# Three feed-forward stages of a hybrid trunk in two phases: first projection by seven block products, second summed in eight banks

## The chip, the cores and the metric

The kernel runs on one core of one Trainium2 chip. The metric is the time of one execution on the device, in microseconds (us). Engines: TensorE (PE, matmuls; PEld its weight loads), VectorE (DVE), ScalarE (ACT), GpSimd (POOL), and SyncE (SP), which here only issues DMAs.

## The reference

Two layers of a trunk over 512 latent tokens and 256 context tokens with width 1024; every layer has a half-step feed-forward network (FFN), a merge of a Fourier and a state-space (S5) branch, and a second half-step FFN. Layer 1 drops the context after its merge, so its last FFN has 512 tokens. Three FFNs have all 768.

```
def swiglu(h, w13, w2):
    a, b = jnp.split(h @ w13, 2, axis=-1)
    return (jax.nn.silu(a) * b) @ w2

def half_ffn(h, g, shift, scale, gate, w13, w2):
    return h + 0.5 * gate * swiglu(modulated_norm(h, g, shift, scale), w13, w2)
```

`w13` is 1024 x 5632 (two outputs a and b of 2816 each), `w2` is 2816 x 1024. Shift, scale and gate are products of a vector with `w_mod` (1024 x 9216 a layer). All is float32.

## The kernel before

Channels lie on partitions. The tokens are two halves (hf 0 and 1) of 384 columns, `HW`. The 2816 inner channels are 22 units of 128 (`NF`). A stage is named layer/FFN: 0/0, 0/2, 1/0 have 768 tokens, 1/2 has 512; merge 0 and merge 1 lie between.

Float32 precision is had from two parts: a value x is a high part (an ACT cast, L203) and a low part (x minus the high part, a VectorE subtraction, L182, rows `wl<-raw,wh` for weights, `s<-u,s` and `g<-u,g` for activations). A product is three matmuls (`mm3`, L207): high x high, weight high x low, weight low x high. A weight chunk is 128 x 1024 (512 KB); SP loads it raw, ACT and VectorE split it. `need` and `take` plan the chunks: one list in the order of use, loaded some chunks ahead, each into one of six slots (`wh0`/`wl0` and so on).

An FFN stage (`ffn`) goes by units: for each half 8 k x 3 matmuls for a and as many for b into PSUM tiles `ab`, then silu on ACT, the product `u<-t,ab` and the split into `g` on VectorE. After each group of two units (`GF`) the second projection of the group before follows: per output block d and half, 2 units x 3 matmuls into an `o` tile, and the residual add `s<-o,mod,s` (L200), two instructions, since latent and context columns have their own gate. The last group is done with the one before it, half by half, so that the norm of half 0 (`sumsq`, `rstd_`, `apply`) lies beside half 1's matmuls. `rstd_` sums over partitions by a matmul with ones (`o<-kc,acc`), computes the root on VectorE and ScalarE, and spreads it with another matmul; `apply` normalizes, modulates and splits x.

Beside that, `gemv` computes the modulation vectors: per chunk of `wm` (128 x 1024, 512 KB, two buffers `gm0`, `gm1`) two VectorE instructions with a running sum (L375) and no matmul. `issue_after` sets it behind the unit's last instruction. In stage 0/0 the hooks issue 56 chunks, in 0/2 72. In 1/0 the hooks issue the S5 parameters (`s5_params`) and eight `s5_ahead`, preparations of the S5 scans on VectorE, one for every second unit. The framework orders each engine's queue; the engines run their queues in order and wait for each other by semaphores.

Of the kernel before, what the change touches and what calls it, by code (L numbers as in the profile page):

```python
# [154 lines left out]
class Net:  # L155
    def __init__(s, tc, ins, out, es):
# [49 lines left out]
    def mm(s, out, w, r, a, z):  # L206
        s.nc.tensor.matmul(out, lhsT=w, rhs=r, start=a, stop=z)  # L207

    def mm3(s, out, w, r, first, last):
        s.mm(out, w[0], r[0], first, False)  # L210
        s.mm(out, w[0], r[1], False, False)
        s.mm(out, w[1], r[0], False, last)
# [221 lines left out]
    def apply(s, l, n, hf, lat, r):  # L434
        nc = s.nc
        h = s.h[hf]
        w = LW if lat else HW
        if not lat:
            xh = s.sb([128, KD, w], s.slab[f"xh{hf}"], F32R)
            xl = s.sb([128, KD, w], s.slab[f"xl{hf}"], F32R)  # L440
            s.x[hf] = lambda k: (xh[:, k, :], xl[:, k, :])
        else:
# [6 lines left out]
        sh, gA = s.mod[l][:, 3 * n], s.mod[l][:, 3 * n + 1]  # L449

        def f(k):
            t, f = s.tmp(w), s.tmp(w, "u")
            s.mul(t, s.cv(h[:, k, :], lat), r)
            for q, sl in s.parts(lat):
                if q == 0:
                    nc.scalar.activation(f[:, sl], t[:, sl], AF.Identity, bias=sh[:, k, q:q + 1], scale=gA[:, k, q:q + 1])
# [771 lines left out]
```

## Time and profile before

| | us |
|---|---|
| time, median of 3 runs | 2867.51 (2866.08 to 2868.71) |
| profiled execution, its own time | 2866.58 |
| its span, first to last instruction | 2864.8 |
| TensorE busy | 2820.2 |
| VectorE busy | 2031.3 |
| ScalarE busy | 889.0 |

The profile is of one execution. Busy shares are averages over stages; by the trace the stages begin at about 25 (0/0), 571 (merge 0), 1016 (0/2), 1575 (1/0), 2164 (merge 1) and 2480 us (1/2). Durations of VectorE instructions overlap by some 0.08 us, so their starts tell more than their ends. DMA share is the mean over 16 DMA engines.

### The profile page before, as it was taken

To read this page: it belongs to the slowest core of one execution; us is meant where nothing else is said; L and a number is where in the kernel's file an instruction comes from. 1 tells how busy PE (TensorE), PEld (TensorE's weight loads), DVE (VectorE), ACT (ScalarE), POOL (GpSimd) and SP (SyncE) were. 2 spreads that over 40 slices of the span, in tenths; PEclk is the share of its full clock that TensorE was granted. 3 is DMA by queue.
4 is the path that set the end of the run, shared out by engine and by line. 5 is a ranking of instruction groups with operands and counts; after the bars stand their busy time and mean duration, and the time that the engine had idled before them with its cause. 6 is when DMAs were issued, how large, how long until landed. Compare 5 with 4: busy or idle time off the path is not lost.

```text
span 2864.8 us, 45267 instructions
## 1 busy us (share of the span) xinstructions
PE 2820.2 (98%) x17704; PEld 2725.6 (95%) x17704; DVE 2031.3 (71%) x4518; ACT 889.0 (31%) x1527; POOL 2.5 (0%) x23
## 2 busy tenths in 40 slices
PE   7999999999999999999999999999999999999998
PEld 6999999999899999999999999999999999988888
DVE  6788785679976668887875757665767878654445
ACT  5221212263344352112122521112135444532222
POOL 0000000000000000000000000000000000000000
PEclk9999999999999999999999999999999999999999
DMA  7444432143433525444441222222225655333321
GB/s 265 154 156 133 153 128 75 50 150 115 124 114 123 162 69 166 160 136 149 150 141 51 74 67 83 87 81 84 98 84 180 194 158 168 100 119 102 96 96 51
DMA packets 139732, 347.02 MB, mean 121 GB/s; under 512 B 23032, under 2 KB 61688, under 8 KB 138752
## 3 DMA queue, kind: packets, MB, share of 16 engines
q1 hardware_dynamic: 139520, 344.13, 36.4%
q8 instruction: 140, 2.29, 0.3%
q14 instruction: 72, 0.59, 0.1%
HBM read 306.98 MB, written 37.09 MB: 120 GB/s over the span
## 4 chain that ended last, share of the span: by engine, by line
PE 86%; DVE 9%; DMA 3%; ACT 1%; issue 1%; SPq 0%; DVEq 0%; ACTq 0%
PE ab L207 58%; PE o L207 27%; DVE g L182 3%; DVE wl L182 2%; DMA gm<-in_wm 1%; DVE q L375 1%; DVE g L832 1%; DMA wl<-vd 1%; ACT wh L203 0%; DVE u L182 0%; DMA wl<-in_wm 0%; PE o L345 0%; DVE s L200 0%; DMA raw<-in_wb 0%; DVE gm L182 0%
## 5 line engine op out<-in xcount | busy, mean ns | idle before, releaser
L207 PE MATMUL ab<-s,wh 128*128 128x384 f32 (+2 forms) x6608 | 1679.1, 333 | 1.5 <-ACT s L203 1.1
L207 PEld LDWEIGHTS ab<-s,wh 128*128 128x128 f32 x6608 | 1180.2, 188 | 26.3 <-issue 3.1
L207 PE MATMUL ab<-s,wl 128*128 128x384 f32 (+2 forms) x3432 | 1137.6, 332 | 0.0
L207 PE MATMUL o<-g,wh 128*128 128x384 f32 (+4 forms) x2656 | 677.7, 338 | 2.9 <-DVE s L200 2.5
L203 ACT CAST wh<-raw 128x1024 fp32r<-128x1024 f32 x356 | 369.0, 1049 | 993.0 <-PE ab L207 426.4
L207 PEld LDWEIGHTS ab<-s,wl 128*128 128x128 f32 x3432 | 645.8, 188 | 11.5 <-issue 1.8
L182 DVE TENSOR_TENSOR wl<-raw,wh 128x1024 fp32r<-128x1024 f32 x356 | 430.8, 1221 | 220.1 <-ACT wh L203 217.0
L200 DVE SCALAR_TENSOR_TENSOR s<-o,mod,s 128x256 f32<-128x256 f32 x1120 | 424.9, 420 | 95.4 <-PE o L207 93.5
L207 PEld LDWEIGHTS o<-g,wh 128*128 128x128 f32 x2656 | 473.1, 188 | 19.3 <-issue 2.2
L207 PE MATMUL o<-g,wl 128*128 128x384 f32 (+4 forms) x1392 | 454.0, 334 | 0.0
L375 DVE SCALAR_TENSOR_TENSOR q<-gm,q 128x1024 f32<-128x1024 f32 x256 | 312.3, 1220 | 27.2 <-DMA gm<-in_wm 24.5
L182 DVE TENSOR_TENSOR u<-t,ab 128x384 f32<-128x384 f32 (+2 forms) x173 | 95.5, 553 | 266.5 <-PE ab L207 265.6
L207 PEld LDWEIGHTS o<-g,wl 128*128 128x128 f32 x1392 | 256.6, 188 | 6.4 <-DVE wl L182 0.8
L203 ACT CAST g<-u 128x384 fp32r<-128x384 f32 (+2 forms) x158 | 81.8, 518 | 277.6 <-DVE u L182 277.3
L494 ACT ACTIVATE t<-ab 128x384 f32<-128x384 f32 (+2 forms) x157 | 77.3, 493 | 259.5 <-PE ab L207 259.4
L207 PE MATMUL ab<-g,wh 128*128 128x384 f32 (+1 forms) x512 | 135.7, 311 | 0.0
L182 DVE TENSOR_TENSOR g<-u,g 128x384 fp32r<-128x384 f32 (+2 forms) x158 | 88.7, 562 | 25.8 <-ACT g L203 25.7
L207 PEld LDWEIGHTS ab<-g,wh 128*128 128x128 f32 x512 | 91.1, 189 | 1.4 <-issue 0.7
L397 ACT ACTIVATE t<-s 128x384 f32<-128x384 f32 (+1 forms) x98 | 47.7, 493 | 94.2 <-DVE s L200 83.3
L207 PE MATMUL ab<-wh,s 128*128 128x256 f32 x400 | 73.0, 283 | 0.0
L182 DVE TENSOR_TENSOR acc<-acc,t 128x384 f32<-128x384 f32 (+1 forms) x98 | 50.7, 518 | 27.9 <-ACT t L397 24.6
L182 DVE TENSOR_TENSOR s<-u,s 128x384 fp32r<-128x384 f32 (+1 forms) x124 | 59.9, 513 | 14.4 <-ACT s L203 13.5
(175 smaller groups left out, 1850.0 us busy)
## 6 DMA issues: line engine op xcount, KB each, us to landing
raw<-in_wa SPq DMA_DIRECT2D x176, 512.0 KB
gm<-in_wm SPq DMA_DIRECT2D x132, 512.0 KB
raw<-in_wb SPq DMA_DIRECT2D x88, 512.0 KB
raw<-in_wgs SPq DMA_DIRECT2D x16, 512.0 KB
raw<-in_wgf SPq DMA_DIRECT2D x16, 512.0 KB
raw<-in_wo SPq DMA_DIRECT2D x16, 512.0 KB
hd<-s SPq DMA_DIRECT2D x4, 1536.0 KB
us<-s SPq DMA_DIRECT2D x16, 320.0 KB
```

The lines of the kernel that those rows point to most:

```text
L182: s.last = s.nc.vector.tensor_tensor(out, a, b, op=op).ins
L200: s.nc.vector.scalar_tensor_tensor(out, a, sc, b, op0=op0, op1=op1)
L203: s.nc.scalar.copy(hi, src)
L207: s.nc.tensor.matmul(out, lhsT=w, rhs=r, start=a, stop=z)
L375: s.nc.vector.scalar_tensor_tensor(s.junk, w, 1.0, s.cb[:, r, :], op0=OP.mult, op1=OP.mult, accum_out=s.raw[:, d, r:r + 1])
L397: nc.scalar.activation(q, src, AF.Square)
L494: nc.scalar.activation(a, pa, AF.Silu)
L832: nc.vector.tensor_tensor_scan(o[:, g, :], rho, a[:, g, :], 0.0, op0=OP.mult, op1=OP.add)
```

## The change

The three 768-token stages become `ffn_two`; stage 1/2 keeps `ffn`.

Phase 1 is the first projection. For a pair of units the weights are a 2 x 2 block matrix (output a or b by half of k), the tokens' x too (X11, X21 of half 0; half 1 enters by sums). Seven products of sums of these blocks stand in place of eight: tokens T1 to T4 and X22 are built once a stage by `apply` of half 1, weights S1 to S4 once a pair on VectorE (`forms`, over raw buffers of their own). A product has two accumulators (units e = 0, 1), 4 k and 3 matmuls each, 24 in all. Each form is a chunk in a ring of five slots. The results of the products are combined by VectorE additions, silu on ACT, and the g of each unit and half goes to DRAM (`gd`). The first two pairs (`FILL`) begin with the products that need half 0 alone (A11x, A12x). h is kept in DRAM meanwhile (`he`).

Phase 2 is the second projection, one half after the other: each half sums all 22 units in eight PSUM banks, one for each d. g is loaded from DRAM and split again (128 x 768, two units), `wb` is loaded for each half again. The last four units (`LAST`) are done d by d with the residual add behind each d. The norm of half 0 is applied during units 3 to 10 of half 1. `gemv` is now one chunk a hook: 22 hooks in phase 1, 44 in phase 2. All S5 parameters and `s5_ahead` of layer 1 lie in phase 2 of stage 1/0, half 0, those of layer 0 in phase 2 of 0/0, half 1.

```diff
+    def wf(w):
+        w = np.asarray(w)
+        w = w.reshape(w.shape[0], 2, 4, 128, 2, NP2, 2, 128)
+        return A(w.transpose(0, 5, 4, 1, 3, 6, 2, 7)).reshape(w.shape[0], NP2, 2, 2, 128, 1024)
+    o["wf0"], o["wf1"] = wf(ffn1_w13), wf(np.asarray(ffn2_w13)[:1])
...
+    def wraw(s, src=None):
+        s.nraw += 1
+        q = s.nraw % 5
+        t = s.sb([128, 1024], "raw", bufs=3) if q < 3 else s.sb([128, 1024], ("wh5", "wl5")[q - 3])
+        if src is not None:
...
+    def forms(s, w):
+        r = {}
+        def tail():
+            r["S1"] = s.wraw()
+            s.add(r["S1"], r["A21"], r["A22"])
+        def a11():
+            for n, (z, k) in (("A11", (0, 0)), ("A21", (1, 0)), ("A22", (1, 1))):
+                r[n] = s.wraw(w[z, k])
+            return r["A11"]
+        def s2():
+            tail()
+            s.sub(r["A21"], r["A11"], r["A21"])
+            s.sub(r["A11"], r["S1"], r["A11"])
+            return r["A11"]
...
+    def order(s):
+        o = [(p, f) for p in range(FILL) for f in ("A11x", "A12x")]
+        o += [(p, "S1f" if p == 0 else "S1a") for p in range(FILL)]
+        for p in range(FILL):
+            o += [(p, f) for f in ("S2l" if p == 0 else "S2a", "S3", "A22", "S4l")]
+        for p in range(FILL, NP2):
...
+            def f(k):
+                j = k % 4
+                if k < 4:
+                    o = h[:, k, :]
+                    modulate(o, k)
+                    s.sub(X[:, k, :], o, X[:, k, :])
+                    s.split(*s.T["T1"](k), X[:, k, :])
+                else:
+                    o, y = s.tmp(w, "u"), s.tmp(w)
+                    modulate(o, k)
+                    s.split(*s.T["X22"](j), o)
+                    s.sub(y, o, X[:, j, :])
+                    s.split(*s.T["T2"](j), y)
+                    s.sub(X[:, j, :], o, h[:, j, :])
+                    s.sub(X[:, k, :], X[:, k, :], y)
+                if k == KD - 1:
+                    t3 = s.sb([128, KD, HW], s.slab["h1"], F32R)
+                    s.T["T3"] = four(t3)
+                    for j in range(4):
+                        s.split(*s.T["T3"](j), X[:, j, :])
+                    for j in range(4):
+                        s.split(*s.T["T4"](j), X[:, 4 + j, :])
+                s.mark = s.last
+            return f
+        if not lat:
+            xh = s.sb([128, KD, w], s.slab[f"xh{hf}"], F32R)
+            xl = s.sb([128, KD, w], s.slab[f"xl{hf}"], F32R)
...
+        def prod(p, f, P, x, first):
+            W = s.take(("wf", l, nn, p, f))
+            for e in range(2):
+                if first:
+                    P[e] = s.ps([128, HW], ("ab", "o")[e])
+                for k in range(4):
+                    sl = slice(512 * e + 128 * k, 512 * e + 128 * k + 128)
+                    s.mm3(P[e], (W[0][:, sl], W[1][:, sl]), s.T[x](k), first and k == 0, k == 3, not first)
+                yield e
...
+            def p6():
+                for e in prod(p, s2, D, "T2", True):
+                    u2[e] = spare()
+                    s.add(u2[e], D[e], a[e])
+            def p7():
+                for e in prod(p, s3, D, "T3", False):
+                    u3[e] = spare()
+                    s.add(u3[e], D[e], a[e])
+                    s.add(u3[e], st["B"][e], u3[e])
+            def p4():
+                for e in prod(p, a22, D, "T4", False):
+                    s.add(a[e], D[e], a[e])
+                    s.mul(s0[e], s0[e], a[e])
+                    nc.sync.dma_start(gd[p][0][:, e], s0[e])
+            def p3():
+                for e in prod(p, s4, st["B"], "X22", False):
+                    s.add(u2[e], st["B"][e], u2[e])
+                    nc.scalar.activation(u2[e], u2[e], AF.Silu)
+                    s.mul(u2[e], u2[e], u3[e])
+                    nc.sync.dma_start(gd[p][1][:, e], u2[e])
...
+        for p in range(FILL, NP2):
+            first(p, st[p])
+            p6, p7, p4, p3 = rest(p, st[p], ("S2", "S3", "A22", "S4"))
+            p6()
+            fifth(p, st[p], "S1")
+            p7()
+            hook(0, 0, 2 * p)
+            second(p, st[p])
+            p4()
+            p3()
+            hook(0, 0, 2 * p + 1)
...
+        T = []
+        for hf in range(2):
+            h = s.h[hf] = s.sb([128, KD, HW], s.slab[f"h{hf}"])
+            nc.sync.dma_start(h, hd[hf])
+            bank = [None] * KD
+            def open_(d):
+                bank[d] = s.ps([128, HW], "ab" if d < 4 else "o")
+            def load_g(p):
+                i = (11 * hf + p) % 2
+                g = s.sb([128, 2, HW], f"g{4 * i}")
+                nc.sync.dma_start(g, gd[p][hf])
+                z = [s.sb([128, 2, HW], f"g{4 * i + 1 + y}", F32R) for y in range(2)]
+                s.split(z[0], z[1], g)
+                return z
+            def step(f, V, g, d, last=False):
+                sl = slice(128 * d, 128 * d + 128)
+                s.mm3(bank[d], (V[0][:, sl], V[1][:, sl]), (g[0][:, f % 2], g[1][:, f % 2]), f == 0, last)
+            take = lambda f: s.take(("wb", l, nn, f, hf))
+            held = []
+            for f in range(NF - LAST):
+                if f % 2 == 0:
+                    g = load_g(f // 2)
+                V = take(f)
+                late = hf == 1 and f < 3
+                for d in range(KD - late):
+                    if f == 0:
+                        open_(d)
+                    step(f, V, g, d)
+                s.mark = s.last
+                if late:
+                    held.append((f, V, g))
+                if hf == 1 and f == 2:
+                    fa = s.apply(ll, ln, 0, False, s.rstd_(T[0], True), two)
+                    with s.tc.issue_after(s.pe):
+                        open_(KD - 1)
+                        for x in held:
+                            step(*x, KD - 1)
+                if hf == 1 and 3 <= f < 3 + KD:
+                    fa(f - 3)
+                hook(1, hf, f)
+            fs = range(NF - LAST, NF)
+            g = {f: load_g(f // 2) for f in fs if f % 2 == 0}
+            V = {f: take(f) for f in fs}
+            for f in fs:
+                hook(1, hf, f)
+            for d in range(KD):
+                for f in fs:
+                    step(f, V[f], g[f - f % 2], d, f == NF - 1)
+                s.resid(l, v, hf, d, bank[d], h[:, d, :], h[:, d, :], False)
+            T.append(s.sumsq(h, False))
...
+        def params(l, n):
+            if n == 0:
+                s.steps = s.s5_params(l)
+            if n >= 0:
                 with s.tc.issue_after(s.mark):
...
+        def hook0(ph, hf, f):
+            s.gemv(1)
+            if ph == 1 and hf == 1:
+                params(0, f - 13)
+        def hook1(ph, hf, f):
+            s.gemv(1)
+        def hook2(ph, hf, f):
+            s.gemv(1)
+            if ph == 1 and hf == 0:
+                params(1, f)
+                if f > 5 and f % 2 == 0:
+                    with s.tc.issue_after(s.mark):
+                        s.s5_ahead(1, f // 2 - 3)
+        s.ffn_two(0, 0, s.i["h"], hook0, (0, 1, False))
+        s.merge(0, False, lambda hf: s.norm(0, 2, hf, False, True))
+        s.gemv_open()
+        s.todo = [(1, v, d) for v in range(9) for d in range(KD)]
+        s.ffn_two(0, 2, None, hook1, (1, 0, True))
+        s.ffn_two(1, 0, None, hook2, (1, 1, False))
+        s.merge(1, True, lambda hf: s.norm(1, 2, hf, True))
+        s.ffn(1, 2, True, lambda f: None, lambda hf: s.final(hf))
```

First place: TensorE in stage 0/0, where the reduction of half 0's squares (`o<-kc,acc`) stands. Before, amid the last unit's first projection of half 1 (`s_313`, `s_314` are high and low x):

```order
L207 MATMUL ab<-s_313,wh_4555 128x384
L207 MATMUL ab<-s_314,wh_4555 128x384
L207 MATMUL ab<-s_313,wl_4556 128x384
L207 MATMUL ab<-s_313,wh_4555 128x384
L207 MATMUL o<-kc,acc 128x1 x3
L207 MATMUL ab<-s_314,wh_4555 128x384
L207 MATMUL ab<-s_313,wl_4556 128x384
L207 MATMUL ab<-s_313,wh_4555 128x384
L207 MATMUL ab<-s_314,wh_4555 128x384
```

After, between the halves of phase 2 (`g_4098`, `g_4282`, `g_4283`: parts of g, the second two of half 1; `wh_3983` is of the last unit of half 0, `wh_4023` of the first of half 1):

```order
L219 MATMUL o<-g_4098,wh_3983 128x384
L219 MATMUL o<-g_4099,wh_3983 128x384
L219 MATMUL o<-g_4098,wl_3984 128x384
L219 MATMUL ab<-g_4282,wh_4023 128x384 x4
L219 MATMUL o<-g_4282,wh_4023 128x384 x3
L219 MATMUL o<-kc,acc 128x1 x3
L219 MATMUL ab<-g_4283,wh_4023 128x384
L219 MATMUL ab<-g_4282,wl_4024 128x384
L219 MATMUL ab<-g_4283,wh_4023 128x384
```

The reduction moved from the middle of a unit of 48 matmuls to behind the first seven of half 1.

Second place: VectorE in the same place, the instructions before the two last sums into acc. Before (`s_65` is h, `q_4704` and `sT` belong to the S5 parameters):

```order
L200 SCALAR_TENSOR_TENSOR s_65<-o,mod_72,s_65 128x256
L182 TENSOR_TENSOR sT<-q_4704 128x32
L182 TENSOR_TENSOR q_4704<-q_4704 128x32
L200 SCALAR_TENSOR_TENSOR s_65<-o,mod_72,s_65 128x128
L182 TENSOR_TENSOR q_4704<-q_4704,sT 128x32
L182 TENSOR_TENSOR acc<-acc,t 128x384
L182 TENSOR_TENSOR sT<-q_4704 128x32
L200 SCALAR_TENSOR_TENSOR s_65<-o,mod_72,s_65 128x256
L182 TENSOR_TENSOR q_4704<-q_4704,sT 128x32
L200 SCALAR_TENSOR_TENSOR s_65<-o,mod_72,s_65 128x128
L182 TENSOR_TENSOR acc<-acc,t 128x384 x3
L197 TENSOR_SCALAR n_5287<-o 128x3
```

After (`s_3408` is h, `gm` a chunk of `wm`, `q_541` a scratch output of the gemv instructions):

```order
L478 SCALAR_TENSOR_TENSOR q_541,gr<-gm_4085,q_538 128x1024
L194 TENSOR_TENSOR wl_4111<-raw,wh_4110 128x1024
L194 TENSOR_TENSOR mod_72<-gr,bm 128x16
L194 TENSOR_TENSOR wl_4117<-raw,wh_4116 128x1024
L478 SCALAR_TENSOR_TENSOR q_541,gr<-gm_4126,q_538 128x1024
L212 SCALAR_TENSOR_TENSOR s_3408<-o,mod_72,s_3408 128x256
L478 SCALAR_TENSOR_TENSOR q_541,gr<-gm_4126,q_538 128x1024
L212 SCALAR_TENSOR_TENSOR s_3408<-o,mod_72,s_3408 128x128
L478 SCALAR_TENSOR_TENSOR q_541,gr<-gm_4131,q_538 128x1024
L194 TENSOR_TENSOR acc<-acc,t 128x384
L478 SCALAR_TENSOR_TENSOR q_541,gr<-gm_4131,q_538 128x1024
L194 TENSOR_TENSOR acc<-acc,t 128x384
```

The residual add of the last d and the sums now stand behind splits of the next half's weights and gemv instructions.

Third place: VectorE in stage 1/0, between two low parts of weights, with the preparations of the S5 scans (`gm` and `q` with 320 and 192 columns). Before, from inside one `s5_ahead`:

```order
L182 TENSOR_TENSOR gm_16795<-q_16305,q_16304 128x192 x2
L182 TENSOR_TENSOR gm_16795<-gm_16795,q_16304 128x192
L182 TENSOR_TENSOR gm_16795<-q_16305,q_16304 128x192
L182 TENSOR_TENSOR q_16304<-q_16305,q_16304 128x192
L182 TENSOR_TENSOR gm_16795<-q_16305,q_16304 128x192
L182 TENSOR_TENSOR gm_16795<-gm_16795,q_16304 128x192
L182 TENSOR_TENSOR g_16872<-u,g_16871 128x384
L182 TENSOR_TENSOR q_16304<-q_16305,q_16304 128x192
L182 TENSOR_TENSOR gm_16795<-gm_16795,q_16304 128x192
L182 TENSOR_TENSOR q_16304<-q_16305,q_16304 128x192
L182 TENSOR_TENSOR gm_16795<-gm_16795,q_16304 128x192
L182 TENSOR_TENSOR wl_16812<-raw,wh_16811 128x1024
```

After, in phase 2, half 0:

```order
L194 TENSOR_TENSOR wl_18379<-raw,wh_18378 128x1024
L194 TENSOR_TENSOR q_17973<-q_17974,q_17973 128x192
L194 TENSOR_TENSOR gm_18353<-q_17973,sBn 128x320
L194 TENSOR_TENSOR gm_18260<-gm_18260,q_17973 128x192
L194 TENSOR_TENSOR gm_18353<-q_17973,sBn 128x320
L194 TENSOR_TENSOR q_17973<-q_17974,q_17973 128x192
L194 TENSOR_TENSOR gm_18260<-gm_18260,q_17973 128x192
L194 TENSOR_TENSOR wl_18415<-raw,wh_18414 128x1024
L194 TENSOR_TENSOR q_17973<-q_17973,sBn 128x320
L194 TENSOR_TENSOR g_18613<-g_18610,g_18612 128x768
L194 TENSOR_TENSOR gm_18346<-q_17973,sbc 128x320 x2
```

The next `s5_ahead` (320 columns) begins before the one ahead of it (192 columns) is through, and the low parts of the weights (`wl`) and of g stand among them.

## Rows read from the trace of the kernel before

**Rows 1.** Page: busy time by engine, granted clock, chain that ended last.

```profile
PE 2820.2 (98%) x17704; PEld 2725.6 (95%) x17704; DVE 2031.3 (71%) x4518; ACT 889.0 (31%) x1527; POOL 2.5 (0%) x23
...
PEclk9999999999999999999999999999999999999999
...
PE 86%; DVE 9%; DMA 3%; ACT 1%; issue 1%; SPq 0%; DVEq 0%; ACTq 0%
```

**Rows 2.** Windows: us, PE PEld DVE ACT POOL busy (count), clock, DMA share, GB/s.

```profile
250.00:300.00 50.00, 50.00 (x287) 49.49 (x286) 40.59 (x78) 9.81 (x14) 0.00 (x0) 1.00 0.44 146
700.00:750.00 50.00, 47.19 (x389) 45.05 (x388) 49.43 (x109) 18.76 (x36) 0.43 (x4) 1.00 0.40 124
1300.00:1350.00 50.00, 50.00 (x287) 49.63 (x286) 40.70 (x79) 9.80 (x14) 0.00 (x0) 1.00 0.44 147
1550.00:1600.00 50.00, 49.96 (x290) 49.36 (x289) 34.38 (x79) 23.26 (x41) 0.00 (x0) 1.00 0.13 43
1950.00:2000.00 50.00, 50.00 (x288) 50.00 (x287) 32.79 (x71) 9.81 (x14) 0.00 (x0) 1.00 0.26 88
```

**Rows 3.** Two windows of the start.

```profile
10.00:31.00 21.00, 13.20 (x105) 8.85 (x105) 11.00 (x30) 8.85 (x18) 0.00 (x0) 1.00 1.01 398
50.00:92.00 42.00, 42.00 (x255) 41.77 (x256) 32.98 (x62) 23.20 (x37) 0.00 (x0) 1.00 0.49 168
```

**Rows 4.** Groups, PE up to 92 us: count | busy, mean ns | idle.

```profile
L207 PE MATMUL ab<-s,wh 128*128 128x384 f32 x166 | 44.8, 349 | 1.1 <-ACT s L203 1.1
L207 PE MATMUL ab<-s,wl 128*128 128x384 f32 x83 | 28.5, 345 | 0.0
L207 PE MATMUL o<-s,wh 128*128 128x384 f32 x32 | 8.0, 337 | 0.0
L207 PE MATMUL o<-s,wl 128*128 128x384 f32 x16 | 5.1, 337 | 0.0
```

**Rows 5.** Groups by shape on VectorE, whole span.

```profile
L182 DVE TENSOR_TENSOR wl<-raw,wh 128x1024 fp32r<-128x1024 f32 x354 | 428.6, 1221 | 215.4 <-ACT wh L203 212.3
L375 DVE SCALAR_TENSOR_TENSOR q<-gm,q 128x1024 f32<-128x1024 f32 x256 | 312.3, 1220 | 27.2 <-DMA gm<-in_wm 24.5
```

**Rows 6.** Timeline, VectorE, stage 0/0: start us, us, instruction, [idle before].

```profile
203.02 1.22 DVE L375 SCALAR_TENSOR_TENSOR q<-gm,q 128x1024 f32<-128x1024 f32 x1
...
204.17 0.56 DVE L182 TENSOR_TENSOR g<-u,g 128x384 fp32r<-128x384 f32 x1
204.64 1.22 DVE L375 SCALAR_TENSOR_TENSOR q<-gm,q 128x1024 f32<-128x1024 f32 x1
...
213.22 0.47 DVE L200 SCALAR_TENSOR_TENSOR s<-o,mod,s 128x256 f32<-128x256 f32 x1
213.62 1.21 DVE L375 SCALAR_TENSOR_TENSOR q<-gm,q 128x1024 f32<-128x1024 f32 x1
...
214.76 0.34 DVE L200 SCALAR_TENSOR_TENSOR s<-o,mod,s 128x128 f32<-128x128 f32 x1
215.02 1.21 DVE L375 SCALAR_TENSOR_TENSOR q<-gm,q 128x1024 f32<-128x1024 f32 x1
...
218.28 1.23 DVE L375 SCALAR_TENSOR_TENSOR q<-gm,q 128x1024 f32<-128x1024 f32 x1 [0.15 <-DMA gm<-in_wm]
```

**Rows 7.** Timeline, queue of SP (issues DMAs), same stretch.

```profile
214.86 3.27 SPq L371 DMA_DIRECT2D gm<-in_wm  x2
```

**Rows 8.** Timeline, VectorE, one s5_ahead in stage 1/0.

```profile
1802.92 0.19 DVE L195 TENSOR_SCALAR sBn<-sbc 128x64 f32<-128x64 f32 x1
...
1809.82 0.94 DVE L182 TENSOR_TENSOR gm<-q,q 128x192 f32<-128x192 f32 x2 [0.38 <-DMA vd<-gm]
...
1814.73 1.22 DVE L182 TENSOR_TENSOR wl<-raw,wh 128x1024 fp32r<-128x1024 f32 x1
```

**Rows 9.** Timeline, VectorE, end of merge 0.

```profile
1016.35 0.74 DVE L200 SCALAR_TENSOR_TENSOR s<-ab,mod,r 128x256 f32<-128x256 f32 x2 [2.21 <-PE ab L207]
```

More of the change, by code (lines that the diff above doesn't have):

```diff
@@ L166, in __init__ @@
         s.spill = {}
+        s.ring, s.nraw, s.first = list(range(RING)), 0, False
     def sb(s, shape, tag, dt=F32, bufs=1, name=None):
@@ L204, in split, with mm, mm3 @@
         s.sub(lo, src, hi.bitcast(F32))
[L206 to L212, printed above, removed]
+    def mm(s, out, w, r, a, z, go_on=False):
+        s.pe = s.nc.tensor.matmul(out, lhsT=w, rhs=r, start=a, stop=z, skip_group_check=go_on).ins
+    def mm3(s, out, w, r, first, last, go_on=False):
+        s.mm(out, w[0], r[0], first, False, go_on)
+        s.mm(out, w[0], r[1], False, False, go_on)
+        s.mm(out, w[1], r[0], False, last, go_on)
     def need(s, key, src, slot, cols=1024):
@@ new lines, in order, with plan_two, need @@
+    def order(s):
[4 more added lines that the diff above has]
+        for p in range(FILL, NP2):
+            o += [(p, f) for f in ("A11", "S2", "S1", "S3", "A12", "A22", "S4")]
+        return o
+    def plan_two(s, l, n):
+        w, b = s.i[f"wf{n}"], s.i[f"wb{n}"]
+        f = [s.forms(w[l, p]) for p in range(NP2)]
+        def need(key, src):
+            s.need(key, src, s.ring[0])
+            s.ring = s.ring[1:] + s.ring[:1]
+        for p, x in s.order():
+            need(("wf", l, n, p, x), f[p][x])
+        for hf in range(2):
+            for k in range(NF):
+                need(("wb", l, n, k, hf), b[l, k])
@@ L437, in apply, with modulate @@
         w = LW if lat else HW
+        sh, gA = s.mod[l][:, 3 * n], s.mod[l][:, 3 * n + 1]
+        def modulate(f, k):
+            t = s.tmp(w)
+            s.mul(t, s.cv(h[:, k, :], lat), r)
+            for q, sl in s.parts(lat):
+                if q == 0:
+                    nc.scalar.activation(f[:, sl], t[:, sl], AF.Identity, bias=sh[:, k, q:q + 1], scale=gA[:, k, q:q + 1])
+                else:
+                    s.ts(f[:, sl], t[:, sl], gA[:, k, q:q + 1], OP.mult, sh[:, k, q:q + 1], OP.add)
+        if two and hf == 1:
+            X = s.X
+            d, x22 = [s.sb([128, KD, HW], s.slab[n], F32R) for n in ("xl1", "h0")]
+            t2, t4 = [[s.sb([128, 2, HW], f"g{o + i}", F32R) for i in range(4)] for o in (0, 4)]
+            four = lambda t: lambda k: (t[:, k, :], t[:, 4 + k, :])
+            two_ = lambda t: lambda k: (t[k // 2][:, k % 2], t[2 + k // 2][:, k % 2])
+            s.T.update(T1=four(d), X22=four(x22), T2=two_(t2), T4=two_(t4))
+            def f(k):
[5 more added lines that the diff above has]
+                    s.split(*s.T["T1"](k), X[:, k, :])
+                else:
+                    o, y = s.tmp(w, "u"), s.tmp(w)
[14 more added lines that the diff above has]
+            return f
         if not lat:
@@ L448, in apply @@
             s.x[hf] = lambda k: [v[:, LW * hf:LW * hf + LW] for v in s.xw(k)]
-        sh, gA = s.mod[l][:, 3 * n], s.mod[l][:, 3 * n + 1]
         def f(k):
[L452 to L456, printed above, removed]
-                else:
-                    s.ts(f[:, sl], t[:, sl], gA[:, k, q:q + 1], OP.mult, sh[:, k, q:q + 1], OP.add)
+            f = X[:, k, :] if two else s.tmp(w, "u")
+            modulate(f, k)
             s.split(*s.x[hf](k), f)
```

190 lines of the change are left out of this document (140 added, 50 removed).

## The prediction, made before the changed kernel had run

> **What bounds the kernel now.** I read the page first. TensorE is busy for 98% of the span, VectorE for 71%, and the chain that ended last is 86% TensorE [rows 1]. Then the windows, to see whether that average holds in each stage. It does: in the three 768-token feed-forward (FFN) stages a 50 us window has 50.00 us of TensorE and 287 or 288 matmuls, so one 128x384 matmul takes 50/287 = 0.1742 us, while VectorE is at 32.8 to 40.7 us [rows 2]. Where VectorE is full (49.43 of 50, in the merge) TensorE drops to 47.19 [rows 2]. So two things decide a stage: how many matmuls it has, and whether VectorE keeps ahead of them. VectorE's instructions overlap a little, so I price them by the distance between starts, the pitch: 1.15 us for 1024 elements, 0.47 for 384, 0.40 and 0.26 for a residual add of 256 and 128 [rows 6]. I use 1.14 for 1024, and 0.87 for 768, an estimate between 384 and 1024.
>
> **What the change removes.** Before, a stage's first projection takes 22 units x 2 halves x 2 outputs x 8 k x 3 = 2112 matmuls. After, 11 pairs x 7 products x 8 x 3 = 1848. Over three stages 3 x 264 = 792 go, x 0.1742 = **138.0 us**, all of it on the full engine [rows 2]. The second projection keeps its count. The sum is made against the profiled execution, 2866.58 us (span 2864.8), 0.93 under the median 2867.51: 2866.6 - 138.0 = 2728.6 if nothing else changes. From here I ask only where TensorE starves.
>
> A rule speaks for stopping at that figure. The Trainium skill, "Perfetto Trace Analysis", section "Identifying the Most-Contended Engine", says to find the engine of highest occupancy and optimize it first; by that alone the time would be 2728.6. Its next section, "Optimization Strategy", speaks against the change: kernels may have several regimes, and interleaving them helps. The trace agrees with the second where it shows VectorE at 99% and TensorE short of full [rows 2].
>
> **Steady stretches.** Phase 1, per pair: TensorE 168 x 0.1742 = 29.3 us. VectorE: 7 low parts, 4 sums of weights and 4 gemv instructions, 15 x 1.14 = 17.1, and 14 x 0.47 = 6.6: 23.7 us, 81%. Stage 0/0 of before ran at 81% with TensorE full [rows 2], so I take 0 of a bound of 3 us a stage. Phase 2, per unit and half: TensorE 24 x 0.1742 = 4.18; VectorE 1.14 + 0.87/2 + 2.28 of gemv = 3.86, 92%. The merge at 99% loses 2.8 us in 50 [rows 2]; 78 units carry a gemv here, 326 us, so by that row the loss is at most 18. But each gemv chunk must land in one of two gm buffers. The row shows an issue at 214.86 and the use at 218.28, 3.4 us [rows 6, 7], and waits for gm of 24.5 us in all [rows 5]. A buffer's round is use (2.3), SP (0 to 1.2) and landing (3.4) = 5.7 to 6.9 us, against two units, 8.36. That fits. I take 4 us of 0 to 20.
>
> **The five places where VectorE starves TensorE.** In each I summed the pitches of all that stands in VectorE's queue up to the operand that TensorE needs, and took off the matmuls that TensorE can still do.
> - Start of 0/0. T1 to T4 now come out of VectorE before the fifth product can start: 17 ops of 1024, 37 of 384 and 6 of 128 are 17 x 1.14 + 37 x 0.47 + 6 x 0.26 = 38.3 us, from about 48.5 us (the last reduction of the modulation), and some 5 of waits: 92 us. By then 192 matmuls (8 products of 24) can be done; before had done 166 + 83 + 32 + 16 = 297 [rows 4], with TensorE full from 50 to 92 [rows 3]. 105 x 0.1742 = **18 us** (14 to 25).
> - Between the halves of phase 2 in 0/0 and 0/2. The reduction `o<-kc,acc` now stands behind seven matmuls of the next unit and ahead of all others, and acc stands on VectorE behind 10 instructions of 1024, the last residual adds and two sums: 10 x 1.14 + 2 x 0.47 + 0.8 = 13.1 us, less 7 x 0.17: **12 us** in 0/0, and 12.5 in 0/2, where the rows are alike. Before, the same reduction stood inside a unit of 48 matmuls with VectorE at 81%, and TensorE stayed full. Bounds 8 to 16 each.
> - From merge 0 into 0/2: VectorE has 19 ops of 1024, 46 of 384 and 8 of 128, 45.8 us with the small ones, from 3.3 us after the last merge matmul (the residual ends about 0.8 after 1016.35 [rows 9], then rstd). TensorE has 8 products, 33.4 us, to do meanwhile. 3.3 + 45.8 - 33.4 = 15.7; some 2.5 of waits between engines: **18** (15 to 23).
> - From 0/2 into 1/0: the same X and T sums, and 10 gemv instructions among them, since the last block of four units puts its hooks there: 30 ops of 1024, 48 of 384, 8 of 128, 60.2 us, against the same 8 products (33.8 with what is left of the last block): 26.4, with waits **29** (26 to 35). Before, VectorE was at 34.4 of 50 there and TensorE full [rows 2].
> - Phase 2 of 1/0. The eight `s5_ahead` and the s5 parameters, spread over the whole stage before, now lie in the 22 units of one half. One `s5_ahead` spans 1802.92 to 1814.73 with two other 384 ops and one short wait inside, so 10.5 us of its own [rows 8]. From the low part of f = 3 to the first of the second half VectorE has 96 ops of 320, 96 of 192 (80.7 us), 23 of 1024 (26.2), 11 of 768 (9.6), 17 of 384 (8.0) and small ones (11.4): 135.9 us. TensorE has 92.3 us of matmuls there, and the weights already split give a lead of 14.2. 135.9 - 106.5 = 29.4. Before, one such block waited 0.38 us for its transfer with others in between [rows 8]; packed, I add 0 to 12 for these and some 4% of pitch: 29 to 49, I take **36**, nearer the bare pitch, since a full VectorE has kept its pitch in the merge.
>
> From 0/0 to merge 0 the last sums of squares are no longer covered by a unit: 2 us (0 to 5).
>
> If TensorE's clock fell after these waits, more would be lost. The row shows it at its full level, 2.4 GHz, in all 40 slices, also in the first, where the engine waited most [rows 1], so I take 0. The Trainium skill, "TensorE: Matmul & The Clock Gate", section "What's actually happening", has the clock fall to half when the array idles. By that rule matmuls between two waits would run at half speed; but they run while VectorE is late, so most of that would cost nothing, and I leave it at 0 to 6.
>
> **Sum.** Given back: 18 + 12 + 12.5 + 18 + 29 + 36 + 2 + 4 = 131.5. 2728.6 + 131.5 = 2860.1, say **2860 us**. With all low ends (14 + 8 + 8 + 15 + 26 + 29) the sum is 100 and the time 2829; with high ends short of the steady ones (25 + 16 + 16 + 23 + 35 + 49 + 5 + 4) it is 173 and 2902.
>
> **The rivals.**
> - The stalls overlap or are shorter: TensorE takes other ready work, or the sums reach it in smaller pieces than I think. For it: VectorE ran at pitch in [rows 6] with no idle time. Against it: both queues are in order, and the same instructions must go through. All terms at bare pitch or lower: 2829 to 2846, say 2838.
> - The full gain: the places above are hidden beside TensorE's other work and cost 0 to 60 us together, 2729 to 2789. By the first of the two rules above this is what comes. Against it stands the arithmetic of 1/0, where 135.9 us of VectorE meets 92.3.
> - Slower, by the transfers of phase 2: each unit and half now moves 0.52 MB of wb, 0.52 of wm and 0.2 of g in 4.18 us, 296 GB/s, where the stages of before moved 146 [rows 2]. At 398 GB/s the queues were full (share 1.01) [rows 3]. If a chunk lands in 6.5 us in place of 3.4, a buffer's round is 2.3 + 0.6 + 6.5 = 9.4 us against 8.36; the gemv instruction waits in VectorE's queue, behind it the low part of the next weights, and TensorE: 0.5 us a unit x 78 = 40, time 2900. It decides from a landing of 5.5 us on.
> - The products don't cut the matmuls: excluded by the instruction list.
>
> **Chances.** Forecast, 2846 to 2876: 0.46. Shorter stalls: 0.24. The full gain: 0.05. Transfers: 0.25. What a measurement of this kernel can tell from no change is about 0.2%, 5.7 us: faster is below about 2861. Of the forecast's 0.46 some 0.20 lies below that, 0.17 within, 0.09 above. Faster: 0.20 + 0.24 + 0.05 = 0.49; same: 0.17; slower: 0.09 + 0.25 = 0.34. The range runs from 2828 to 2902: it leaves out the full gain (0.05), a little below (0.04) and the end of the transfers' case (0.08).
>
> **What would show it.** The profile after should have about 16,900 matmuls, 792 fewer; VectorE's busy share higher (its pitches sum to 2111 us in place of 1865); TensorE's share near 94%; TensorE full in 50 us windows of phase 1; VectorE at 95% or more in windows at the two entries and in the first half of phase 2 of 1/0, with TensorE waiting for VectorE's `wl` and `s` there for 25 to 50 us each. I'd be wrong if those windows had TensorE full, if the granted clock fell after them, or if VectorE waited for gm by much more than the 24.5 us of now.

## The result: slower by 1.5%, and the profile after

The changed kernel took 2909.53 us (median of 4 runs, 2906.79 to 2914.17) against 2866.8 before: a ratio of 1.0151, 95% interval 1.0133 to 1.0168. The forecast was 2860, the range ended at 2902. In the profiled execution the span grew from 2864.8 to 2908.2, by 43.4 us.

The page after, engines, granted clock and chain, against [rows 1]:

```profile
PE 2735.4 (94%) x16912; PEld 2622.3 (90%) x16912; DVE 2259.7 (78%) x4302; ACT 1092.9 (38%) x1725; POOL 2.5 (0%) x23
...
PEclk9999998999999999999989799999899999999999
...
PE 77%; DVE 16%; DMA 4%; issue 2%; ACT 1%; SPq 0%; DVEq 0%; ACTq 0%
```

The 792 matmuls are gone (17704 to 16912). But the chain that ended last is now 16% VectorE, in place of 9%, and the clock row, all nines before, has four slices below. Then the windows (same columns as [rows 2]): a steady one in each phase, the stretches in which the prediction had looked for waits, and, in a fence of its own, the start in the kernel before.

```profile
250.00:300.00 50.00, 50.00 (x289) 50.00 (x288) 41.22 (x57) 17.98 (x24) 0.00 (x0) 1.00 0.36 117
400.00:450.00 50.00, 50.00 (x289) 50.00 (x288) 47.70 (x68) 17.03 (x18) 0.00 (x0) 1.00 0.88 296
...
0.00:125.00 125.00, 96.44 (x678) 83.19 (x679) 100.87 (x202) 64.05 (x109) 0.81 (x7) 0.97 0.61 216
450.00:575.00 125.00, 102.86 (x530) 100.31 (x529) 103.48 (x182) 42.92 (x58) 0.00 (x0) 0.88 0.65 220
1025.00:1100.00 75.00, 64.15 (x333) 59.98 (x333) 69.03 (x130) 42.13 (x74) 0.00 (x0) 0.89 0.34 113
1450.00:1600.00 150.00, 124.62 (x666) 121.81 (x665) 126.13 (x213) 51.78 (x70) 0.00 (x0) 0.90 0.68 225
1600.00:1700.00 100.00, 80.81 (x410) 77.35 (x409) 91.51 (x154) 42.02 (x66) 0.00 (x0) 0.85 0.41 137
1975.00:2150.00 175.00, 137.44 (x738) 133.39 (x737) 160.68 (x420) 60.88 (x84) 0.00 (x0) 0.89 0.56 191
```

```profile
0.00:125.00 125.00, 105.36 (x773) 97.25 (x774) 90.48 (x211) 53.23 (x93) 0.81 (x7) 1.00 0.64 228
```

In both phases, steady, TensorE is full: 289 matmuls in 50 us, at 0.173 us each, even where the transfers run at 296 GB/s and VectorE is busy for 95%. So the products save what they should. In each stretch below the first two, what is lost is the stretch less count x 0.1742; for the start it is the matmuls that are missing against the kernel before, x 0.1742:

| stretch | what it is | forecast | lost |
|---|---|---|---|
| to 125 us | start of 0/0 (678 matmuls by then, 773 before: 95 fewer) | 18 | 16.5 |
| 450 to 575 | halves of phase 2, 0/0 | 12 | 32.7 |
| 1025 to 1100 | from merge 0 into 0/2 | 18 | 17.0 |
| 1450 to 1600 | halves of phase 2, 0/2 | 12.5 | 34.0 |
| 1600 to 1700 | from 0/2 into 1/0 | 29 | 28.6 |
| 1975 to 2150 | phase 2 of 1/0 | 36 | 46.4 |
| steady, end of 0/0, rest | | 6 | 6.2 (what is left) |

The last row is what is left of 181.4, the 138.0 that the fewer matmuls save and the 43.4 by which the span grew. Four of the six places came out as forecast within 2 us or within their bounds (phase 2 of 1/0: 29 to 49). The two boundaries between the halves lost 66.7 in place of 24.5: 42 of an error of 50 us.

What stands there, on TensorE in 0/0 (timeline: start us, us, instruction, [idle before <- releaser]):

```profile
473.17 0.34 PE L219 MATMUL o<-g,wl 128*128 128x384 f32 x1
475.95 1.65 PE L219 MATMUL ab<-g,wh 128*128 128x384 f32 x4 [2.44 <-ACT g L215]
477.40 1.16 PE L219 MATMUL o<-g,wh 128*128 128x384 f32 x3
486.80 1.41 PE L219 MATMUL o<-kc,acc 128*128 128x1 f32 x6 [8.24 <-DVE acc L194]
488.07 0.67 PE L219 MATMUL ab<-g,wh 128*128 128x384 f32 x1
488.54 0.52 PE L219 MATMUL ab<-g,wl 128*128 128x384 f32 x1
488.86 0.52 PE L219 MATMUL ab<-g,wh 128*128 128x384 f32 x1
...
500.03 0.83 PE L219 MATMUL o<-kc,n 128*128 128x128 f32 x6
```

The waits for g and acc are the 12 us of the forecast (2.4 + 8.2 and the slow matmuls between). After the wait the matmuls start 0.32 us apart in place of 0.174: the clock has fallen to its lower level, 1.2 GHz, half of full speed, as the window there shows:

```profile
480.00:490.00 10.00, 3.20 (x12) 3.23 (x13) 8.91 (x16) 1.80 (x2) 0.00 (x0) 0.50 0.93 343
```

What the forecast hadn't seen is the second half of the stretch. TensorE's waits in 440 to 575 us:

```profile
PE ab L219 <- DVE g L194: 11.5, 3, 6.1
PE o L219 <- DVE acc L194: 8.2, 1, 8.2
PE ab L219 <- ACT g L215: 2.4, 1, 2.4
```

and VectorE in the same time:

```profile
494.19 1.22 DVE L478 SCALAR_TENSOR_TENSOR q<-gm,q 128x1024 f32<-128x1024 f32 x1
495.34 0.08 DVE L478 DVE_READ_ACCUMULATOR q<-gm,q 128x1 f32 x1
501.41 1.03 DVE L194 TENSOR_TENSOR t<-s,acc 128x384 f32<-128x384 f32 x2 [5.99 <-ACT acc L525]
502.35 0.60 DVE L209 TENSOR_SCALAR u<-t,mod 128x128 f32<-128x128 f32 x2
```

VectorE, which everything waits for, stood idle itself for 6.0 us: its next instruction needs the spread root, whose matmul (`o<-kc,n`, at 500.03) stands in TensorE's queue behind units that were late. Then `apply` (three instructions a unit) and gemv (two) and the split of weights and g keep it above TensorE's pace, and TensorE waits three times for g.

Of the 32.7 us lost in this stretch TensorE's waits are 22.1 (2.4 + 8.2 + 11.5). Of the other 10.6 some 8 lie in about 54 matmuls behind the waits that start 0.32 us apart. Waits for a transfer are small: 2.6 us of VectorE for gm (440 to 575), 0.8 us of ScalarE for wb (470 to 575).

### The profile page after: what moved, and what is told of

It reads as the page before. It is cut to its first block, busy times and chain, and to the rows that moved or that the text cites. A ratio compares the mean times of both kernels' runs of the same rounds, so it can differ in the third digit from the quotient of the medians.

```text
span 2908.2 us, 44175 instructions
## 1 busy us (share of the span) xinstructions
PE 2735.4 (94%) x16912; PEld 2622.3 (90%) x16912; DVE 2259.7 (78%) x4302; ACT 1092.9 (38%) x1725; POOL 2.5 (0%) x23
## 4 chain that ended last, share of the span: by engine, by line
PE 77%; DVE 16%; DMA 4%; issue 2%; ACT 1%; SPq 0%; DVEq 0%; ACTq 0%
PE ab L219 46%; PE o L219 31%; DVE g L194 4%; DVE wl L194 4%; DVE q L478 2%; DVE s L194 2%; DVE gm L194 1%; DMA gm<-in_wm 1%; DVE t L194 1%; DMA wl<-vd 1%; DVE g L1149 1%; DVE q L194 1%; DMA vd<-gm 0%; ACT wh L215 0%; DVE raw L194 0%
## 5 line engine op out<-in xcount | busy, mean ns | idle before, releaser
L219 PE MATMUL ab<-s,wh 128*128 128x384 f32 (+2 forms) x3736 | 948.2, 332 | 16.7 <-DVE s L194 11.7
L219 PEld LDWEIGHTS ab<-s,wh 128*128 128x128 f32 x3736 | 663.5, 190 | 45.1 <-issue 15.8
L194 DVE TENSOR_TENSOR wl<-raw,wh 128x1024 fp32r<-128x1024 f32 (+1 forms) x423 | 515.0, 1221 | 235.0 <-ACT wh L215 230.4
L219 PE MATMUL ab<-s,wl 128*128 128x384 f32 (+2 forms) x1996 | 657.1, 329 | 0.6 <-DVE wl L194 0.6
L219 PE MATMUL ab<-g,wh 128*128 128x384 f32 (+1 forms) x2096 | 560.9, 338 | 76.7 <-DVE g L194 56.0
L219 PEld LDWEIGHTS ab<-g,wh 128*128 128x128 f32 x2096 | 385.8, 192 | 92.0 <-DVE g L194 62.9
L219 PE MATMUL o<-s,wh 128*128 128x384 f32 (+3 forms) x1496 | 380.1, 335 | 0.1
L219 PE MATMUL ab<-g,wl 128*128 128x384 f32 (+1 forms) x920 | 313.7, 341 | 1.6 <-DVE wl L194 1.6
L219 PEld LDWEIGHTS o<-s,wh 128*128 128x128 f32 (+1 forms) x1496 | 268.7, 188 | 3.0 <-ACT u L1378 0.8
L212 DVE SCALAR_TENSOR_TENSOR s<-o,mod,s 128x256 f32<-128x256 f32 x208 | 88.3, 463 | 26.0 <-PE o L219 24.8
```

The source lines that it names most:

```text
L194: s.last = s.nc.vector.tensor_tensor(out, a, b, op=op).ins
L212: s.nc.vector.scalar_tensor_tensor(out, a, sc, b, op0=op0, op1=op1)
L219: s.pe = s.nc.tensor.matmul(out, lhsT=w, rhs=r, start=a, stop=z, skip_group_check=go_on).ins
```

## The experiments

**1. The S5 preparations in phase 1 of 1/0, where VectorE has room.**

```diff
-            if ph == 1 and hf == 0:
-                params(1, f)
-                if f > 5 and f % 2 == 0:
+            if ph == 0:
+                params(1, f - 2)
+                if f > 6 and f % 2 == 1:
                     with s.tc.issue_after(s.mark):
-                        s.s5_ahead(1, f // 2 - 3)
+                        s.s5_ahead(1, (f - 7) // 2)
```

(and six chunks of gemv go from 1/0 into phase 1 of 0/2: `s.gemv(2 if ph == 0 and f < 6 else 1)` in its hook.)

> The S5 parameters and the eight s5_ahead of layer 1 lie in phase 1 of stage 1/0 (units 2 to 21) in place of phase 2; six gemv chunks move from 1/0 into phase 1 of 0/2. Theory (VectorE's queue starves TensorE where its work is packed): the waits of phase 2 of 1/0 (41 us between 1980 and 2160, and 5.5 us of matmuls at half clock) go, phase 1 of 1/0 has VectorE at about 92% and loses 0 to 8 us. 2868 us (2860 to 2877). Rival (the transfers of phase 2, or its eight banks, set the pace): TensorE stays as starved there without this work: 2900 or more. Second rival (phase 1 can't hide it either): the loss moves, 2895 to 2910.

2885.36 us, ratio 1.0067 (1.0052 to 1.0082): 24 us gained where 41 were expected, outside the range of the theory and of both rivals. The place is right, the hiding isn't complete. Phase 1 of 1/0 and the end of phase 2 (windows):

```profile
1725.00:1975.00 250.00, 244.11 (x1375) 238.74 (x1374) 234.78 (x471) 86.28 (x117) 0.00 (x0) 1.00 0.42 138
1975.00:2050.00 75.00, 75.00 (x430) 74.72 (x429) 40.87 (x55) 26.11 (x29) 0.00 (x0) 1.00 0.67 234
2050.00:2100.00 50.00, 43.94 (x227) 42.75 (x226) 29.34 (x55) 21.94 (x33) 0.00 (x0) 0.90 0.46 163
```

Phase 1 has VectorE at 94% and loses 250 - 1375 x 0.1742 = 10.5 us; the boundary between the halves keeps 10.5. The 75 us of phase 2 before that boundary are full (430 matmuls at 234 GB/s), so its banks and the transfers of wb and g don't bound it.

**2. No gemv at the boundaries.**

```diff
-            s.gemv(1)
+            if ph == 0:
+                s.gemv(2)          # 0/0: 2 if f < 14 else 1
+            elif 11 * hf <= f < NF - LAST:
+                s.gemv(1)
```

> No gemv in the blocks of the last four units and in units 0 to 10 of half 1 of stages 0/0 and 0/2; phase 1 takes two chunks a unit instead (0/0: for 14 units). Theory: the acc of half 0 comes some 11 us earlier at both boundaries, units 3 to 10 of half 1 fit (VectorE 1.14 + 0.44 + 1.3 = 2.9 us a unit against 4.18), and the entry into 1/0 loses 10 instructions of 1024. Of 51 us of waits and 14 us at half clock at the boundaries some 45 go, 11 at the entry; phase 1 at 97% of VectorE costs 5 to 15. 2862 us (2850 to 2876). Rival (transfers set phase 2): wb and g are the same, the boundaries keep their waits, 2900 or more. Rival (clock first): the waits halve but the clock still falls at both places; 2885.

2893.1 us, ratio 1.0092 (1.0077 to 1.0107): 16 us gained, 47 expected. The windows at the boundaries and at four other places:

```profile
120.00:180.00 60.00, 54.09 (x296) 53.30 (x295) 58.22 (x92) 16.56 (x24) 0.00 (x0) 0.94 0.58 185
450.00:575.00 125.00, 116.09 (x638) 114.16 (x637) 88.99 (x180) 50.03 (x67) 0.00 (x0) 0.95 0.57 193
1025.00:1200.00 175.00, 160.56 (x863) 155.25 (x862) 164.61 (x267) 70.39 (x107) 0.00 (x0) 0.93 0.48 155
1360.00:1410.00 50.00, 42.08 (x209) 40.41 (x208) 39.52 (x63) 13.53 (x19) 0.00 (x0) 0.86 0.88 314
1450.00:1600.00 150.00, 141.06 (x782) 139.17 (x781) 109.85 (x177) 59.06 (x80) 0.00 (x0) 0.95 0.59 198
1580.00:1690.00 110.00, 99.49 (x523) 95.38 (x522) 98.37 (x164) 50.01 (x76) 0.00 (x0) 0.91 0.41 134
```

The boundaries now lose 13.9 and 13.8 us, 39 less than with gemv in them. So gemv there was the larger part of what they cost, and wb and g, which are unchanged, were not. (The transfers of wm moved with gemv, but the waits for a transfer given above for 0/0, 3.4 us in all, are too small for its share of the 39.) The entry into 1/0, with ten gemv instructions fewer ahead of it, loses 18.9 in place of 28.6 (last row). But twice the gemv in phase 1 isn't free as "5 to 15" had it: 8.4 us at 120 to 180, 13.6 where phase 1 of 0/2 ends (1360 to 1410), and 24.7 in 1025 to 1200, where the changed kernel lost 17.0 up to 1100 and under 1 after. The mechanism was confirmed and its price elsewhere underrated.

**3. Both.**

```diff
-            elif 11 * hf <= f < NF - LAST:
+            elif 11 * hf <= f < (NF if hf else NF - LAST):
                 s.gemv(1)
```

(in 0/2, so that the last chunks are done before the S5 work begins; the other edits are those of 1 and 2)

> Both edits of e1_s5_early and e2_gemv_away, with all gemv chunks of layer 1 done in stage 0/2. Theory: the gains add up, 2822 us (2808 to 2838), faster than the kernel before. Rivals (transfers, or a phase 1 that is full): 2870 or more.

2872.84 us, ratio 1.0022 (1.0013 to 1.0032). That is 51 us above the 2822 expected and in the range of the rivals. The gains add (24 + 16 = 40, measured 37), and the prices that experiments 1 and 2 showed in phase 1 remain: of the rivals, a phase 1 that is too full fits.

**4. Half 0's norm at every second unit.**

```diff
-                if hf == 1 and 3 <= f < 3 + KD:
-                    fa(f - 3)
+                if hf == 1 and f > 2 and f % 2 == 1:
+                    fa((f - 3) // 2)
```

> The eight steps of half 0's norm in phase 2, half 1, at every second unit (3, 5, ... 17) in place of units 3 to 10. Theory: VectorE needs 3.86 + 1.3 = 5.2 us a unit in units 3 to 10 against 4.18 of TensorE; spaced, 4.5: of the 8 us and the half clock behind them in each of 0/0 and 0/2 most goes, the first wait at acc stays: 2892 us (2882 to 2902). Rival (the copy of the root that comes late on ScalarE, 6 us of idle VectorE at 501, or transfers, set it): 2905 to 2912.

2895.84 us, ratio 1.0103 (1.0088 to 1.0118): 14 us gained, within 4 of what was expected, while the first wait, for acc, stays. The two boundaries (the second window lies 10 us earlier, since 0/0 is shorter):

```profile
450.00:575.00 125.00, 107.70 (x587) 106.10 (x585) 111.54 (x228) 46.59 (x63) 0.00 (x0) 0.92 0.68 230
1440.00:1590.00 150.00, 129.22 (x700) 126.59 (x699) 133.54 (x224) 51.40 (x69) 0.00 (x0) 0.92 0.73 240
```

They lose 22.7 and 28.1, 10.0 and 5.9 less than in the changed kernel. So units 3 to 10 of half 1, where `apply` meets gemv, were a loss of their own, in two stages.

**5 and 8. The weight sums on GpSimd**, alone and with the spread of experiment 7.

```diff
-            s.add(r["S1"], r["A21"], r["A22"])
+            s.nc.gpsimd.tensor_tensor(r["S1"], r["A21"], r["A22"], op=OP.add)
```

(and so for S2, S3, S4.)

> The sums of weight blocks (S1 to S4, four of 128x1024 a pair) are computed on GpSimd in place of VectorE; all else as in the changed kernel. Theory (VectorE's queue at the entries is the price): some 6 to 8 of these sums stand in VectorE's queue at each of the three entries, 7 to 9 us each, so the entries lose 15 to 25 us less in all; in phase 1 nothing changes, TensorE was full there. 2888 us (2880 to 2898). Rival (the sums are on the path either way, and GpSimd, of which no row here shows a speed, is slower at them): the entries wait for GpSimd: 2910 to 2950. Rival (what bounds the entries is the token sums, not the weights): no change, 2905 to 2912.

> The spread of e7_spread with the weight sums on GpSimd as in e5_pool_sums. Theory: both gains, and phase 1 has more room (VectorE 65% without gemv's second chunk): 2815 us (2800 to 2835). If GpSimd is slow at the sums: as e5 against the changed kernel, 0 to 40 over e7.

2973.66 (ratio 1.0377, 1.0362 to 1.0391) and 2979.99 (1.0396, 1.0381 to 1.0410): the rival of a slow GpSimd, and beyond its range. A sum there takes 2.5 us or more; one of VectorE's instructions beside it grew to nearly three times its length. GpSimd, then VectorE:

```profile
290.19 2.60 POOL L265 TENSOR_TENSOR raw<-raw 128x1024 f32<-128x1024 f32 x1 [10.35 <-issue]
```

```profile
290.44 3.43 DVE L481 SCALAR_TENSOR_TENSOR q<-gm,q 128x1024 f32<-128x1024 f32 x1
293.81 0.08 DVE L481 DVE_READ_ACCUMULATOR q<-gm,q 128x1 f32 x1
293.92 1.22 DVE L481 SCALAR_TENSOR_TENSOR q<-gm,q 128x1024 f32<-128x1024 f32 x1
```

Counted in the two timelines, 44 gemv instructions lay beside one of GpSimd's and took 2.84 us on average, the 212 others 1.22. The chain load, sum, cast, low part is longer too: TensorE waits 23.9 us for high parts of weights (`wh`), 1.8 in the changed kernel.

**6 and 9. The wait filled with matmuls.** 48, then 78 matmuls more stand between the halves of phase 2 in all three stages; their output is overwritten.

```diff
+            dum = s.pe
...
+                    if f == 0 and hf == 1 and d == 0:
+                        with s.tc.issue_after(dum):
+                            for _ in range(48):        # 78 in the second
+                                s.mm(bank[0], s.T0[0], s.T0[1], True, True)
...
+            s.T0 = (V[NF - 1][0][:, 0:128], g[NF - 2][0][:, 1])
```

> 48 matmuls of 128x384 more (8.4 us at full clock) stand in TensorE's queue between the two halves of phase 2, in each of the three stages, ahead of the first matmul of half 1; their results are overwritten. They fill a wait for acc of 11 to 13 us. Theory (waits set the time, the half clock behind them costs a few us where TensorE has work ready): the clock stays up, some 20 matmuls a place run at 0.174 in place of 0.32: 2 to 3 us a place less: 2903 us (2898 to 2908). Rival (the half clock costs nothing since VectorE is late anyway): 2909 to 2912. Rival (TensorE was not free there): 2918 to 2935.

> As e6_filled_wait with 78 matmuls in place of 48 between the halves of phase 2: 13.6 us, which closes the wait for acc in 0/0 (5.1 us were left with 48, and the clock still fell). Theory (half clock costs what the ready matmuls behind the wait lose): some 18 matmuls a place at 0.174 in place of 0.32, 2.6 us a place, up to 8 in all: 2902 to 2907. Rival (VectorE is late behind them anyway): 2908 to 2912 with full clock in the window. Rival (the extra work delays half 1): 2915 or more.

2909.85 us (ratio 1.0157, 1.0143 to 1.0171) and 2917.47 (1.0180, 1.0165 to 1.0195), against 1.0151 without. 144 matmuls more, 25 us of TensorE's work, cost nothing that can be measured: TensorE had that much room in its waits. 234, 41 us, cost some 8, in the range of experiment 9's last rival, that the extra work delays half 1. With 78 TensorE waits no longer for acc in 0/0, and the clock stays at 2.4 GHz up to 485 us; then it falls twice (windows of 10 us):

```profile
475.00:485.00 10.00, 10.00 (x60) 10.00 (x59) 9.57 (x17) 3.01 (x5) 0.00 (x0) 1.00 0.69 228
485.00:495.00 10.00, 7.97 (x37) 7.65 (x36) 8.39 (x13) 3.06 (x3) 0.00 (x0) 0.83 0.83 296
...
515.00:525.00 10.00, 4.12 (x13) 3.88 (x13) 9.22 (x17) 2.52 (x4) 0.00 (x0) 0.51 0.87 289
```

But experiment 9 changed more than the wait. In 0/0 and 0/2 the reduction for acc now stands behind the first units of half 1, in 0/0 at 503.27 us in place of 486.80, and VectorE waits for it (TensorE's row, then VectorE's wait):

```profile
503.27 0.72 PE L219 MATMUL o<-kc,acc 128*128 128x1 f32 x6
```

```profile
DVE n L209 <- PE o L219: 7.7, 1, 7.7
```

So the two experiments show that TensorE has room at the boundaries. They don't show what the half clock costs: counted in the timelines, 217 and 227 matmuls of 128x384 start at least 0.30 us apart in them, 228 in the changed kernel and 15 in the kernel before. The half clock was moved, not lessened.

**7. VectorE's work spread by its room.** gemv twice a unit only in units 5 to 18 of phase 1 of 0/0 and 6 to 18 of 0/2, none at the boundaries, twelve chunks in phase 1 of 1/0, and the S5 work behind them: five `s5_ahead` in phase 1, three in phase 2.

```diff
+            if ph == 0:                                # 0/2; 4 < f < 19 in 0/0
+                s.gemv(2 if 5 < f < 19 else 1)
+            elif 11 * hf <= f < NF - LAST:
+                s.gemv(1)
...
+            if ph == 0:                                # 1/0
+                s.gemv(2 if f > 1 else 0)
+                params(1, f - 8)
+                if f > 12 and f % 2 == 1:
+                    with s.tc.issue_after(s.mark):
+                        s.s5_ahead(1, (f - 13) // 2)
+            if ph == 1 and hf == 0 and f in (3, 9, 15):
+                with s.tc.issue_after(s.mark):
+                    s.s5_ahead(1, 5 + f // 6)
```

> VectorE's work spread by its room: gemv twice a unit only in the middle of phase 1 (units 5 to 18 in 0/0, 6 to 18 in 0/2), none in the last blocks nor in units 0 to 10 of half 1; twelve chunks in phase 1 of 1/0; there the S5 parameters and five s5_ahead behind them, three in half 0 of phase 2. Theory: as both edits together (2872.8), less 8 us at the start of phase 1 of 0/0 and of 0/2 each, 13 at the end of phase 1 of 0/2 and 9 at the entry into 1/0: 2840 us (2830 to 2852). Rival (phase 1 can't take twice the gemv anywhere): 2865 to 2885.

2836.88 us (2835.46 to 2839.05), ratio to before 0.9900 (0.9887 to 0.9914): 73 us less than the changed kernel with the same instructions on TensorE, and faster than both. Its page:

```profile
PE 2721.9 (96%) x16912; PEld 2608.8 (92%) x16912; DVE 2242.9 (79%) x4302; ACT 1091.9 (39%) x1727; POOL 2.5 (0%) x23
...
PE 81%; DVE 13%; DMA 2%; issue 2%; ACT 2%; SPq 1%; DVEq 0%; ACTq 0%
```

VectorE executes as many instructions as in the changed kernel, 4302; only their places differ. A steady window of phase 1 has VectorE at 98% with TensorE full:

```profile
250.00:300.00 50.00, 50.00 (x288) 50.00 (x287) 48.98 (x74) 17.62 (x24) 0.00 (x0) 1.00 0.52 163
1575.00:1630.00 55.00, 44.31 (x211) 40.63 (x211) 51.60 (x90) 28.50 (x47) 0.00 (x0) 0.81 0.35 110
```

Its span is 31.0 us shorter than before (2864.8 to 2833.8), so 107 of the 138.0 us are still lost. About half of that is at the three entries (second row: 18.2 us into 1/0).

**10. Four `s5_ahead` in each phase of 1/0.**

```diff
-                if f > 12 and f % 2 == 1:
+                if 12 < f < 20 and f % 2 == 1:
...
-            if ph == 1 and hf == 0 and f in (3, 9, 15):
+            if ph == 1 and hf == 0 and f in (1, 5, 9, 13):
                 with s.tc.issue_after(s.mark):
-                    s.s5_ahead(1, 5 + f // 6)
+                    s.s5_ahead(1, 4 + f // 4)
```

> As e7_spread, but four s5_ahead in phase 1 of 1/0 (units 13 to 19) and four in half 0 of phase 2 (units 1, 5, 9, 13), in place of five and three. Theory: the 10 us wait at the change from phase 1 to phase 2 of 1/0 in e7_spread comes from VectorE's backlog and goes, phase 2 has room (10.5 us of work against 4 x 2.6 us of slack in four units): 2829 us (2824 to 2834). Rival (that wait is for the store and load of g): 2835 to 2840.

2841.79 us, ratio 0.9928 (0.9915 to 0.9941): not faster than experiment 7, and above both ranges that were put up for it. The change of phase and the rest of half 0 of phase 2, in experiment 7 and then here:

```profile
1915.00:1945.00 30.00, 21.48 (x115) 20.98 (x114) 18.49 (x34) 7.13 (x8) 0.00 (x0) 0.89 0.72 248
1960.00:2060.00 100.00, 94.67 (x523) 92.49 (x522) 73.41 (x137) 42.32 (x58) 0.00 (x0) 0.97 0.58 198
```

```profile
1915.00:1945.00 30.00, 24.63 (x131) 24.13 (x130) 15.57 (x26) 8.50 (x10) 0.00 (x0) 0.89 0.68 251
1960.00:2060.00 100.00, 87.14 (x477) 84.71 (x476) 75.50 (x145) 38.31 (x52) 0.00 (x0) 0.95 0.56 194
```

The change of phase loses 7.2 us in place of 10.0, so one `s5_ahead` fewer ahead of it was worth 2.8 us; what sets the rest stays open. Phase 2 and its boundary lose 16.9 in place of 8.9: they had no room for the fourth `s5_ahead` where it was put.

## Why the prediction was wrong

- **What is removed**: right. 792 matmuls at 0.174 us; TensorE is full in both steady phases.
- **Steady phases, and the rival of the transfers**: it was right to put the loss low, and the rival, with its 0.25, fell. At 296 GB/s, as worked out, TensorE lost nothing (window 400 to 450), and VectorE's instructions waited for gm for 7.9 us in all, less than the 24.5 of [rows 5]. Of the way to "slower" only the sign was right.
- **The entries**: right within 2 us (16.5, 17.0, 28.6 for 18, 18, 29). Summing the pitches of an in-order queue up to the operand that is needed, less the matmuls at hand, gave the time. (The operations listed for 1/0 sum to 58.8, not 60.2; nothing hangs on it.)
- **Phase 2 of 1/0**: 46.4 for 36, inside its 29 to 49. The boundary between the halves lies in that stretch too, and had no term of its own. In experiment 1, without the S5 work, it cost 10.5 us; if the two add, 35.9 are left for the S5 work, and the 36 was right for it.
- **Between the halves, 12 and 12.5: the step that failed.** The sum stopped at acc. Measured are 32.7 and 34.0. The wait for acc was sized right (2.4 + 8.2 us). Behind it come the 6.0 us in which VectorE waits for the spread root, and units 3 to 10, where VectorE has 3.86 + 1.2 us a unit against 4.18: TensorE waits another 11.5 us for g. Some 8 us more, in 0/0, lie in matmuls at the lower clock, which the sum had at 0. That units 3 to 10 are too full follows from rows that stood there: 3.86 was worked out for a phase 2 with gemv, and `apply`'s three instructions (0.47 + 0.26 + 0.47) were counted at the entries, but nobody added them in the units where both fall. Experiment 2 takes 39 us off the two boundaries by moving gemv alone, experiment 4 takes 14 off by spacing `apply` alone.
- **The clock**: the prediction took 0 here, and this failed too. The trace has four of 40 slices below full, and 0.50 of full speed, 1.2 GHz, at 480 to 490 us. Some 213 matmuls more than before (228 less 15) start about 0.32 us apart in place of 0.174: 213 x 0.146 = 31 us. The rule cited for it from the Trainium skill, "TensorE: Matmul & The Clock Gate", section "What's actually happening", that the clock falls when the array idles, agrees with the trace. How much of the 31 us the time would lose at full clock stays open, and so does the reasoning that matmuls between two waits cost little at half clock: no run lessens them alone.
- **The cause of the loss**: by experiment 7, with the same matmuls and the same number of VectorE's instructions, 73 us of it was VectorE's work at the wrong places. That is more than the 43 us by which the change is slower. Whether the 107 us that stay lost there are a matter of places or of the amount of VectorE's work, no run here tells.

Of the error of 50 us in the profiled execution (2866.6 + 43.4 - 2860.1) 42 are the two boundaries and 10 phase 2 of 1/0, less 3 at the other places.
